# Stages of two attention heads, and transposes of four norm blocks, at one place between weight tiles

## The chip, the core and the metric

The kernel runs on one core of a Trainium2 chip. TensorE (PE in the profile, PEld its weight loads) multiplies, VectorE (DVE) and ScalarE (ACT) work on tiles, and SyncE (SP) issues the transfers; each engine takes its own instructions strictly in the order in which the program lists them. The metric is the device time of one execution in microseconds. Before the change it is 2163.51 us, the median of three runs (2163.22 to 2163.67).

## What is computed

Two layers of a decoder trunk, on 256 tokens of width 2048, in float32. Cut to what matters:

```python
for l in range(2):
    h = rms_norm(x, norm_mix[l])
    proj = h @ w_in[l]
    o_a = diff_attention(...)       # 4 heads: (softmax(q1 k1) - lam * softmax(q2 k2)) @ v, then an RMS norm over each head
    o_b = forgetting_attention(...) # 6 heads, logits += cumsum(log f)[t] - cumsum(log f)[s]
    o_c = latent_attention(...)     # 6 heads, q and kv from low-rank parts
    x = x + concat(o_a, o_b, o_c) @ w_out[l]
    h = rms_norm(x, norm_ffn[l])
    x = x + square(relu(h @ w_ff_up[l])) @ w_ff_down[l]
```

## The kernel before

Every weight matrix passes once through the chip in tiles of 128 rows and up to 1024 columns. `load_w` (L187) fetches a tile (`wraw`), rounds it on ACT to a high part (`whi`, L194) and leaves the rest on DVE as a low part (`wlo`, L195); there are three buffers for each part. A product of float32 quality is made of three passes on PE: high by high, high by the activations' low part, and low by high. For a tile of 1024 columns that is 12 matmuls of 512 columns, called `wo`, `dn` and so on after their accumulator; the products of one layer are, in order, the input projections (`mq`, `mkv`, `fv`, `fq`, `fk`, `dq`, `dk`, `dv`), the output projection (`wo`), and the two of the feed-forward part (`u`, `dn`).

All else is background work. A stage is a Python generator, cut by `yield` into portions. The class `Background` (L81) holds a queue of them. After each weight tile the program calls `bg.step()` (L100), which credits 1.25 units (never over 4 in hand) and runs one portion for each whole unit. So background work is written between weight tiles, and a scheduler below the program then places it on each engine, near where it was written. `bg.finish()` (L106) runs all that is left at once.

`side_by_side` (L111) joins several stages into one, two of them active: it takes a portion of the first, yields, takes one of the second, yields. It carries the heads: `latent_head` (L567) and `fox_head` (L652) have five portions each (scale; transposes of q and k, `qk`; scores `s` and their exponentials, `exps` L368; transposes of the probabilities, `pt`, from `transposed_p` L385; values `o`), `diff_maps` (L717) four (transposes `qk`; scores of the first map; scores of the second and their difference; `pt`). The last portion of a head ends the generator without a yield, so that it costs no unit.

The end of differential attention matters below. `diff_values` (L742) of a head makes its output `o` on PE; then, for each of the two row blocks, ACT squares it (L751) and DVE copies it to `osb` (L752). `diff_outputs` (L755) makes from the sums of squares of all four heads the norm's factors (`rsqrt_of` L212: eleven small DVE operations, `a_subln`, `y_subln`, `w_subln`), multiplies both `osb` (L760), transposes them on PE (`qk`), and splits the result to the last four heads' slots of `mix` (`split_to` L202). These slots are what the last four of the 16 weight tiles of the left half of `wo` multiply (`HEAD_ORDER` puts these heads last). The left half runs 12 tiles with `bg.step`, then `bg.finish()`, then the last four (L786 to L790):

```python
out_columns(left, w_left, 0, HALF, 0, N_EARLY, bg.step)
bg.finish()
out_columns(left, w_left, 0, HALF, N_EARLY, 16)
```

`Norm.columns` (L277) prepares the activations of the next product: squares on ACT for the norm, then for each pair of 128-column blocks four transposes into one bank (`xt`) and the split of both blocks, with a yield after each pair.

Of the kernel before, what the change touches and what calls it, by code (L numbers as in the profile page):

```python
# [19 lines left out]
P = 128  # L20
D_MODEL = 2048
SEQ = 256
# [5 lines left out]
NH_A, NH_B, NH_C = 4, 6, 6  # L28
# [52 lines left out]
class Background:  # L81

    def __init__(self):
        self.tasks = deque()
        self.rate = 1.25
        self.due = 0.0
# [11 lines left out]
    def step(self):  # L100
        self.due = min(self.due + self.rate, 4.0)
        while self.due >= 1.0:
            self.due -= 1.0
            self.one()

    def finish(self):  # L106
        while self.tasks:
# [2 lines left out]

def side_by_side(stages, width=2):  # L111

    rest, active = deque(stages), []
    while rest or active:
        while rest and len(active) < width:
            active.append(rest.popleft())
        for a in list(active):
            try:
                next(a)
                yield  # L120
            except StopIteration:
                active.remove(a)


@with_exitstack
def trunk_kernel(ctx: ExitStack, tc: tile.TileContext, ins: dict, out: bass.AP):
# [10 lines left out]
    def acc_tile(name):  # L137
        return ps_acc.tile([P, 512], F32, tag="acc", name=name)

    def t_tile(name):  # L140
        return ps_t.tile([P, 512], F32, tag="t", name=name)

    def mm(out, lhsT, rhs, start, stop):
        nc.tensor.matmul(out, lhsT, rhs, start=start, stop=stop)  # L144

    bg = Background()
# [23 lines left out]
    x = cp.tile([P, NT, D_MODEL], F32, name="x")  # L170
# [10 lines left out]
    for j in range(4):  # L181
        h = cp.tile([P, SEQ], F32, name=f"half{j}")
# [16 lines left out]
    def parts_tile(tag, name):  # L199
        return hp.tile([P, 2, 2, SEQ], F32R, tag=tag, name=name)  # L200

    def split_to(dst, src, gain):  # L202

        if gain is None:
            nc.scalar.activation(dst[:, 0, :], src, AF.Copy)
            nc.vector.tensor_tensor(dst[:, 1, :], src, dst[:, 0, :], ALU.subtract)
        else:
            nc.scalar.activation(dst[:, 0, :], src, AF.Copy, scale=gain)  # L208
            nc.vector.scalar_tensor_tensor(dst[:, 1, :], src, gain, dst[:, 0, :], ALU.mult, ALU.subtract)


    def rsqrt_of(ss, n, spans, name):  # L212
        a = sp.tile([P, 48], F32, tag="rs_a", name=f"a_{name}")
        y = sp.tile([P, 48], F32, tag="rs_y", name=f"y_{name}", bufs=3)
        w = sp.tile([P, 48], F32, tag="rs_w", name=f"w_{name}")
        for sl, d in spans:
            nc.vector.tensor_scalar(a[:, sl], ss[:, sl], 1.0 / d, EPS, ALU.mult, ALU.add)
        nc.vector.tensor_scalar(y[:, :n].bitcast(I32), a[:, :n].bitcast(I32), -0.5, RSQRT_SEED, ALU.mult, ALU.add)
        for _ in range(3):
            nc.vector.tensor_tensor(w[:, :n], y[:, :n], y[:, :n], ALU.mult)  # L220
            nc.vector.scalar_tensor_tensor(w[:, :n], w[:, :n], -0.5, a[:, :n], ALU.mult, ALU.mult)
            nc.vector.scalar_tensor_tensor(y[:, :n], w[:, :n], 1.5, y[:, :n], ALU.add, ALU.mult)
        return y
# [45 lines left out]
    class Norm:  # L269
# [7 lines left out]
        def columns(self, c0, n):  # L277
            for q in range(c0 // 512, (c0 + n) // 512):
                for t in range(NT):
                    junk = sp.tile([P, 512], F32, tag="junk", name="junk")  # L280
                    nc.scalar.activation(junk, x[:, t, q * 512:(q + 1) * 512], AF.Square, accum_out=self.sums[:, t, q:q + 1])
            for k in range(c0 // P, (c0 + n) // P, 2):
                b = acc_tile("xt")
                for i in range(2):
                    for t in range(NT):
                        transpose_block(b[:, i * SEQ + t * P:i * SEQ + (t + 1) * P], x[:, t, (k + i) * P:(k + i + 1) * P])
                h = parts_tile("ht", "ht")
                for i in range(2):
                    split_to(h[:, i], b[:, i * SEQ:(i + 1) * SEQ], self.gain[:, k + i:k + i + 1])
                self.h.append(h)  # L290
                yield

        def scale(self):

# [59 lines left out]
    def transpose_block(dst, src):  # L354
        nc.tensor.transpose(dst, src, ident)  # L355
# [45 lines left out]
    def heads_transposed(pairs):  # L401

        b = t_tile("qk")
        for i, blocks in enumerate(pairs):
            for t in range(NT):
                transpose_block(b[:, i * SEQ + t * P:i * SEQ + (t + 1) * P], blocks[t])
        return b
# [12 lines left out]
    h = norm.h  # L420

    for l in range(DEPTH):
# [18 lines left out]
        def mix_slot(i):  # L441

            return mix[i // 2][:, i % 2]
# [150 lines left out]

        mix_slots()
        bg.add(latent_rotation(), side_by_side([latent_head(i) for i in range(NH_C)]))


# [76 lines left out]
        def fox_half(s):  # L675
            qk = [ap.tile([P, 768], F32, tag="mid", name=f"fqk{s}{t}", bufs=4) for t in range(NT)]
            ss = sp.tile([P, 12], F32, tag="ss_f", name="ss_f")
            for a, g in enumerate(("fq", "fk")):
                if l == 0:
                    cols = slice((2 * s + a) * 512, (2 * s + a + 1) * 512)  # L680
                    nc.sync.dma_start(x[:, :, cols], ins["x"][:, :, cols])
                w_in_group(l, f"{g}{s}", h, scaled_copy(lambda t: qk[t][:, a * 384:(a + 1) * 384]))
                for t in range(NT):
                    head_sums(ss[:, t * 6 + 3 * a:t * 6 + 3 * a + 3], qk[t][:, a * 384:(a + 1) * 384], 3, P)
            rf = rsqrt_of(ss, 12, [(slice(0, 12), P)], f"fox{s}")
            bg.add(side_by_side([fox_head(i, qk, rf) for i in range(3 * s, 3 * s + 3)]))
# [30 lines left out]
        def diff_maps(i):  # L717
# [16 lines left out]
            dpT[i] = transposed_p(p1)  # L734

        bg.add(diff_rotation(), side_by_side([diff_maps(i) for i in range(NH_A)]))
        w_in_group(l, "dv", h, scaled_copy(lambda t: dv[t]))

# [3 lines left out]
        def diff_values(i):  # L742
            pT = dpT[i]
            o = t_tile("o")
            vi = slice(i * P, (i + 1) * P)
            mm(o[:, :P], pT[:, :P], dv[0][:, vi], True, True)
            mm(o[:, P:SEQ], pT[:, P:2 * P], dv[0][:, vi], True, False)
            mm(o[:, P:SEQ], pT[:, 2 * P:], dv[1][:, vi], False, True)
            for t in range(NT):
                junk = sp.tile([P, 512], F32, tag="junk", name="junk")  # L750
                nc.scalar.activation(junk[:, :P], o[:, t * P:(t + 1) * P], AF.Square, accum_out=ss_o[:, t * 4 + i:t * 4 + i + 1])  # L751
                nc.vector.tensor_copy(osb[t][:, vi], o[:, t * P:(t + 1) * P])  # L752
            yield

        def diff_outputs():  # L755
            ro = rsqrt_of(ss_o, 8, [(slice(0, 8), P)], "subln")
            yield
            for t in range(NT):
                o3 = osb[t].rearrange("p (n d) -> p n d", d=P)
                nc.vector.tensor_tensor(o3, o3, ro[:, t * 4:(t + 1) * 4].unsqueeze(2).broadcast_to([P, 4, P]), ALU.mult)  # L760
            yield
            for i in range(0, NH_A, 2):
                b = heads_transposed([[osb[t][:, (i + a) * P:(i + a + 1) * P] for t in range(NT)] for a in range(2)])
                for a in range(2):
                    split_to(mix_slot(12 + i + a), b[:, a * SEQ:(a + 1) * SEQ], g_o)
                yield

        bg.add(*(diff_values(i) for i in range(NH_A)), diff_outputs())


        if l + 1 < DEPTH:
# [2 lines left out]
        h = norm.h  # L774
# [3 lines left out]
        def out_columns(accs, w, c0, width, first, last, step=lambda: None):  # L778
            per = 1024 // width
            for i in range(first, last, per):  # L780
                hi, lo = load_w(w(i // per), 1024)
                for k in range(per):
                    product_x(accs, heads[i + k], hi, lo, k * width, i + k == 0, i + k == 15)
                step()
# [8 lines left out]
        for q in range(2):  # L793
            c0 = HALF + q * 512
# [96 lines left out]
        banks = [t_tile, acc_tile]  # L891
# [86 lines left out]
def build(shapes):  # L978
    import concourse.bacc as bacc

    nc = bacc.Bacc("TRN2", target_bir_lowering=False, num_devices=1, dynamic_dma_scratch_size=1024)
    ins = {k: nc.dram_tensor(f"in_{k}", s, F32, kind="ExternalInput").ap() for k, s in shapes.items()}
    out = nc.dram_tensor("out_0", (SEQ, D_MODEL), F32, kind="ExternalOutput").ap()
    with tile.TileContext(nc) as tc:
        trunk_kernel(tc, ins, out)
    return nc
# [9 lines left out]
```

## Time and profile before

| | before |
|---|---|
| median of three runs | 2163.51 us |
| the profiled execution's own time | 2162.75 us |
| its span, first to last instruction | 2161.0 us |
| PE busy | 2147.7 us, 99% of the span |
| PE weight loads busy | 1858.4 us, 86% |
| DVE busy | 1358.7 us, 63% |
| ACT busy | 1082.2 us, 50% |
| DMA, mean share of 16 engines | 57.4% (weights) |

The time of an execution and the span of its trace differ by 1.75 us that lie around the first and the last instruction. Busy time of PE counts a matmul from its start to a modelled end, and matmuls overlap in the pipeline, so the pace of PE is read from the starts of its rows, not from their lengths.

### The profile page before, as it was taken

The numbers are of one execution on the slowest core, as the hardware profiler recorded it, in microseconds if no ns is written. First come the engines' busy times: TensorE is split into PE (matmuls) and PEld (weight loads), VectorE is DVE, ScalarE is ACT, GpSimd is POOL, SyncE is SP. The second block draws the span as 40 slices with busy tenths as digits, with TensorE's granted clock in tenths as the row PEclk, the third lists the DMA queues.
The fourth block names the chain that finished last, engine by engine and source line by source line (L and its number), as shares of the span: only waits on it lengthen the run. The fifth ranks groups of instructions, "written<-read, shape, count | busy, mean of one in ns | idle before, by whom it ended". The sixth has DMA issues, their size and how long they took to land. (4 is left out here: it accounts for less than half of the span.)

```text
span 2161.0 us, 29221 instructions
## 1 busy us (share of the span) xinstructions
PE 2147.7 (99%) x11080; PEld 1858.4 (86%) x11080; DVE 1358.7 (63%) x2160; ACT 1082.2 (50%) x1603; POOL 13.5 (1%) x16
## 2 busy tenths in 40 slices
PE   9999999999999999999999999999999999999999
PEld 7999888888888888888899998888888888888887
DVE  7876676656565655555668667766555555655654
ACT  6655555544454444544566555555444444444442
POOL 2000000000000000000000000000000000000000
PEclk9999999999999999999999999999999999999999
DMA  8545545555566566655555455455565666655654
GB/s 277 173 140 179 163 150 181 186 193 189 193 189 193 185 196 193 189 192 190 184 161 171 137 182 172 146 184 185 186 195 185 195 193 189 193 189 191 193 190 153
DMA packets 115420, 395.68 MB, mean 183 GB/s; under 512 B 13008, under 2 KB 13136, under 8 KB 115280
## 3 DMA queue, kind: packets, MB, share of 16 engines
q1 hardware_dynamic: 115280, 393.83, 57.4%
q8 instruction: 86, 1.41, 0.3%
q14 instruction: 54, 0.44, 0.1%
HBM read 391.68 MB, written 2.10 MB: 182 GB/s over the span
## 5 line engine op out<-in xcount | busy, mean ns | idle before, releaser
L195 DVE TENSOR_TENSOR wlo<-wraw,whi 128x1024 fp32r<-128x1024 f32 (+3 forms) x773 | 909.0, 1178 | 707.5 <-ACT whi L194 694.8
L194 ACT ACTIVATE whi<-wraw 128x1024 fp32r<-128x1024 f32 (+3 forms) x773 | 788.5, 1021 | 954.7 <-PE dn L144 354.5
L144 PE MATMUL u<-ht,whi 128*128 128x512 f32 x2048 | 513.0, 392 | 0.0
L144 PE MATMUL dn<-whi,g 128*128 128x512 f32 x2048 | 510.5, 390 | 0.4 <-ACT whi L194 0.4
L144 PEld LDWEIGHTS dn<-whi,g 128*128 128x128 f32 x2048 | 383.1, 188 | 79.7 <-issue 1.2
L144 PEld LDWEIGHTS u<-ht,whi 128*128 128x128 f32 x2048 | 369.2, 189 | 66.7
L144 PEld LDWEIGHTS u<-ht,wlo 128*128 128x128 f32 x2048 | 279.4, 190 | 20.0
L144 PE MATMUL u<-ht,wlo 128*128 128x256 f32 x2048 | 285.5, 282 | 0.0
L144 PE MATMUL dn<-wlo,g 128*128 128x512 f32 x1024 | 277.3, 389 | 0.0
L144 PEld LDWEIGHTS dn<-wlo,g 128*128 128x128 f32 x1024 | 192.3, 188 | 40.0
L144 PE MATMUL wo<-whi,mix 128*128 128x512 f32 x512 | 138.1, 400 | 0.5 <-ACT mix L208 0.5
L144 PEld LDWEIGHTS wo<-whi,mix 128*128 128x128 f32 x512 | 94.3, 188 | 19.4 <-ACT mix L208 0.9
L323 DVE TENSOR_TENSOR x<-dn,x 128x512 f32<-128x512 f32 x128 | 79.7, 684 | 26.1 <-PE dn L144 26.1
L144 PE MATMUL wo<-wlo,mix 128*128 128x512 f32 x256 | 74.1, 390 | 0.0
L375 ACT ACTIVATE p<-p,nm 128x128 f32<-128x128 f32 x80 | 35.8, 448 | 44.6 <-DVE nm L374 44.6
L144 PEld LDWEIGHTS wo<-wlo,mix 128*128 128x128 f32 x256 | 48.0, 188 | 10.4
L144 PE MATMUL fq<-whi,ht 128*128 128x384 f32 x256 | 53.7, 349 | 0.0
L827 DVE TENSOR_TENSOR relu<-u,relu 128x256 f32<-128x256 f32 x128 | 53.4, 418 | 0.0
L144 PE MATMUL fk<-whi,ht 128*128 128x384 f32 x256 | 51.7, 343 | 0.0
L144 PE MATMUL fv<-whi,ht 128*128 128x384 f32 x256 | 51.1, 340 | 0.0
L826 ACT COPY relu<-u 128x256 f32<-128x256 f32 x128 | 45.9, 359 | 0.0
L828 DVE SCALAR_TENSOR_TENSOR relu<-relu,rsb 128x512 f32<-128x512 f32 x64 | 44.3, 692 | 2.3
(252 smaller groups left out, 1671.5 us busy)
## 6 DMA issues: line engine op xcount, KB each, us to landing
wraw<-in_w_up SPq DMA_DIRECT2D x256, 512.0 KB, 4.2
wraw<-in_w_down_a SPq DMA_DIRECT2D x128, 512.0 KB, 4.2
wraw<-in_w_down_b SPq DMA_DIRECT2D x112, 512.0 KB, 3.6
wraw<-in_w_out_a SPq DMA_DIRECT2D x32, 512.0 KB, 3.6
wraw<-in_w_out_b SPq DMA_DIRECT2D x32, 512.0 KB, 3.5
wraw<-in_w_fv SPq DMA_DIRECT2D x32, 384.0 KB, 3.1
wraw<-in_w_fq SPq DMA_DIRECT2D x32, 384.0 KB, 3.2
wraw<-in_w_fk SPq DMA_DIRECT2D x32, 384.0 KB, 3.1
```

Source lines behind the costliest of these rows:

```text
L144: nc.tensor.matmul(out, lhsT, rhs, start=start, stop=stop)
L194: nc.scalar.activation(hi[:, cols], raw[:, cols], AF.Copy)
L195: nc.vector.tensor_tensor(lo[:, cols], raw[:, cols], hi[:, cols], ALU.subtract)
L323: nc.vector.tensor_tensor(cols, acc, cols, ALU.add)
L375: nc.scalar.activation(p[:, cols], p[:, cols], AF.Exp, bias=nm[:, i:i + 1], scale=-1.0, accum_out=z[:, i:i + 1])
L826: nc.scalar.copy(r[:, cols], u[i][:, SEQ:])
L827: nc.vector.tensor_tensor(r[:, cols], u[i][:, :SEQ], r[:, cols], ALU.add)
L828: nc.vector.scalar_tensor_tensor(r, r, 0.0, rsb2, ALU.max, ALU.mult)
```

## The change

A background step now runs a round. `side_by_side` takes one portion of every active stage and then yields how many there were; `Background.step` takes what a step yields off the credit (1 for a stage that yields nothing), so that a round of two costs two units and the credit may fall below zero. A stage whose generator ends is found by the default that `next` returns, and the round in which it ends is paid like the others. The values of the four differential heads, which stood in the queue one by one, go through `side_by_side` too, and lose their yield. `Norm.columns` transposes four blocks into two banks in one step of two units and then splits all four. Nothing is added to or taken from the arithmetic.

```diff
     def step(self):
         self.due = min(self.due + self.rate, 4.0)
         while self.due >= 1.0:
-            self.due -= 1.0
-            self.one()
+            self.due -= self.one() or 1.0
...
 def side_by_side(stages, width=2):
     rest, active = deque(stages), []
     while rest or active:
         while rest and len(active) < width:
             active.append(rest.popleft())
-        for a in list(active):
-            try:
-                next(a)
-                yield
-            except StopIteration:
-                active.remove(a)
+        n = len(active)
+        active = [a for a in active if next(a, active) is not active]
+        yield n
...
-            for k in range(c0 // P, (c0 + n) // P, 2):
-                b = acc_tile("xt")
-                for i in range(2):
+            for k in range(c0 // P, (c0 + n) // P, 4):
+                banks = [acc_tile("xt") for _ in range(2)]
+                for i in range(4):
                     for t in range(NT):
-                        transpose_block(b[:, i * SEQ + t * P:i * SEQ + (t + 1) * P], x[:, t, (k + i) * P:(k + i + 1) * P])
-                h = parts_tile("ht", "ht")
-                for i in range(2):
-                    split_to(h[:, i], b[:, i * SEQ:(i + 1) * SEQ], self.gain[:, k + i:k + i + 1])
-                self.h.append(h)
-                yield
+                        transpose_block(banks[i // 2][:, i % 2 * SEQ + t * P:i % 2 * SEQ + (t + 1) * P],
+                                        x[:, t, (k + i) * P:(k + i + 1) * P])
+                for j, b in enumerate(banks):
+                    h = parts_tile("ht", "ht")
+                    for i in range(2):
+                        split_to(h[:, i], b[:, i * SEQ:(i + 1) * SEQ], self.gain[:, k + 2 * j + i:k + 2 * j + i + 1])
+                    self.h.append(h)
+                yield 2
...
                 nc.vector.tensor_copy(osb[t][:, vi], o[:, t * P:(t + 1) * P])
+            return
             yield
...
-        bg.add(*(diff_values(i) for i in range(NH_A)), diff_outputs())
+        bg.add(side_by_side([diff_values(i) for i in range(NH_A)]), diff_outputs())
```

What this does to the order of the instructions is shown at three places; numbers behind names are buffer numbers, and line numbers of the changed kernel are one or two off.

The first is PE in layer 1, at the end of differential attention, from the next to last stage of values on (`wo` are the weight tiles' matmuls, `o` a head's values, `qk` the transposes of the normed outputs `osb`). Before:

```order
L144 MATMUL wo<-whi,mix_4_10281 128x512 x8
L144 MATMUL wo<-wlo,mix_4_10281 128x512 x4
L144 MATMUL o<-dv_12152,pT 128x128 x2
L144 MATMUL o<-dv_12153,pT 128x128
L144 MATMUL wo<-whi,mix_5_10282 128x512 x8
L144 MATMUL wo<-wlo,mix_5_10282 128x512 x4
L144 MATMUL wo<-whi,mix_5_10282 128x512 x8
L144 MATMUL wo<-wlo,mix_5_10282 128x512 x4
L355 MATMUL qk<-cst,osb_12368 128x128 x2
L355 MATMUL qk<-cst,osb_12369 128x128
```

And with the change:

```order
L142 MATMUL o<-dv_12152,pT 128x128 x2
L142 MATMUL o<-dv_12153,pT 128x128
L142 MATMUL wo<-whi,mix_5_10282 128x512 x8
L142 MATMUL wo<-wlo,mix_5_10282 128x512 x4
L142 MATMUL o<-dv_12152,pT 128x128 x2
L142 MATMUL o<-dv_12153,pT 128x128
L142 MATMUL o<-dv_12152,pT 128x128 x2
L142 MATMUL o<-dv_12153,pT 128x128
L355 MATMUL qk<-cst,osb_12368 128x128 x2
L355 MATMUL qk<-cst,osb_12369 128x128
```

Before, two weight tiles (24 matmuls) stand between the last head's values and the transposes; now the values of the last two heads stand directly ahead of the transposes. In layer 0 the same two tiles have gone from between them.

The second is DVE at the same place in layer 1 (`osb` are the copies, `wlo` the low part of a weight tile, `subln` the small operations of the norm's factors). Before:

```order
L752 COPY osb_12368<-o 128x128
L752 COPY osb_12369<-o 128x128
L195 TENSOR_TENSOR wlo<-wraw,whi 128x1024
L752 COPY osb_12368<-o 128x128
L752 COPY osb_12369<-o 128x128
L217 TENSOR_SCALAR a_subln<-ss_o 128x8
L218 TENSOR_SCALAR y_subln<-a_subln 128x8
L220 TENSOR_TENSOR w_subln<-y_subln 128x8
L221 SCALAR_TENSOR_TENSOR w_subln<-w_subln,a_subln 128x8
L222 SCALAR_TENSOR_TENSOR y_subln<-w_subln,y_subln 128x8
```

And with the change:

```order
L193 TENSOR_TENSOR wlo<-wraw,whi 128x1024
L752 COPY osb_12368<-o 128x128
L752 COPY osb_12369<-o 128x128
L752 COPY osb_12368<-o 128x128
L752 COPY osb_12369<-o 128x128
L215 TENSOR_SCALAR a_subln<-ss_o 128x8
L216 TENSOR_SCALAR y_subln<-a_subln 128x8
L218 TENSOR_TENSOR w_subln<-y_subln 128x8
```

One `wlo` now stands ahead of four copies instead of two, and the norm's eleven small operations follow them; the second `wlo`, which stood among the eleven, has moved ahead.

The third is PE in layer 1 at the second pair of differential heads (`s` are the scores, `pt` the transposes of the probabilities). Before:

```order
L144 MATMUL s<-kT,half_102 128x128
L144 MATMUL s<-kT,half_102 128x256
L144 MATMUL wo<-whi,mix_3_10280 128x512 x8
L144 MATMUL wo<-wlo,mix_3_10280 128x512 x4
L144 MATMUL s<-kT,half_106 128x128
L144 MATMUL s<-kT,half_106 128x256
L144 MATMUL wo<-whi,mix_3_10280 128x512 x8
L144 MATMUL wo<-wlo,mix_3_10280 128x512 x4
L355 MATMUL pt<-cst,p 128x128 x3
L144 MATMUL wo<-whi,mix_4_10281 128x512 x3
L355 MATMUL pt<-cst,p 128x128
```

And with the change:

```order
L142 MATMUL s<-kT,half_102 128x128
L142 MATMUL s<-kT,half_102 128x256
L142 MATMUL s<-kT,half_106 128x128
L142 MATMUL s<-kT,half_106 128x256
L142 MATMUL wo<-whi,mix_4_10281 128x512 x8
L142 MATMUL wo<-wlo,mix_4_10281 128x512 x4
L355 MATMUL pt<-cst,p 128x128
L142 MATMUL wo<-whi,mix_4_10281 128x512
L355 MATMUL pt<-cst,p 128x128 x2
L142 MATMUL wo<-whi,mix_4_10281 128x512 x7
L142 MATMUL wo<-wlo,mix_4_10281 128x512 x2
L355 MATMUL pt<-cst,p 128x128
```

The scores of the two heads, which stood on either side of a weight tile, now stand together; one tile separates them from the transposes of the first head as it separated the second head's scores from the first head's transposes before, and the transposes of the second head come within that next tile.

## Rows read from the trace of the kernel before

**Rows 1.** The page: busy time by engine, clock granted in 40 slices.

```profile
PE 2147.7 (99%) x11080; PEld 1858.4 (86%) x11080; DVE 1358.7 (63%) x2160; ACT 1082.2 (50%) x1603; POOL 13.5 (1%) x16
...
PEclk9999999999999999999999999999999999999999
```

**Rows 2.** Waits of PE, whole span: total us, times, longest.

```profile
PE fv L144 <- DVE wlo L195: 0.8, 2, 0.4
...
PE pt L355 <- DVE p L731: 0.6, 3, 0.2
```

**Rows 3.** Timeline of PE, 136 to 148 us: start, length, what, count.

```profile
138.69 0.49 PE L355 MATMUL pt<-cst,p 128*128 128x128 f32 x3
...
141.11 1.47 PE L144 MATMUL o<-pT,mv 128*128 128x256 f32 x8
142.33 1.66 PE L144 MATMUL fv<-whi,ht 128*128 128x384 f32 x8
...
146.60 0.83 PE L144 MATMUL cum<-cst,lfx 128*128 128x128 f32 x6
```

**Rows 4.** Timeline of all engines, layer 1, end of differential attention.

```profile
1382.80 0.83 PE L144 MATMUL o<-dv,pT 128*128 128x128 f32 x6
1383.38 2.09 PE L144 MATMUL wo<-whi,mix 128*128 128x512 f32 x8
1383.72 0.28 ACT L751 ACTIVATE junk<-o 128x128 f32<-128x128 f32 x1 [0.58 <-PE o L144]
...
1384.31 0.28 DVE L752 COPY osb<-o 128x128 f32<-128x128 f32 x1
...
1385.03 0.29 DVE L752 COPY osb<-o 128x128 f32<-128x128 f32 x1 [0.43 <-ACT junk L751]
...
1385.24 0.16 DVE L217 TENSOR_SCALAR a_subln<-ss_o 128x8 f32<-128x8 f32 x1
...
1387.90 0.16 DVE L220 TENSOR_TENSOR w_subln<-y_subln 128x8 f32<-128x8 f32 x1
...
1388.49 1.29 DVE L760 TENSOR_TENSOR osb<-osb,y_subln 128x512 f32<-128x512 f32 x2
1389.24 0.44 PE L355 MATMUL qk<-cst,osb 128*128 128x128 f32 x2
...
1389.84 0.88 PE L355 MATMUL qk<-cst,osb 128*128 128x128 f32 x6 [0.17 <-DVE osb L760]
...
1390.95 2.14 PE L144 MATMUL wo<-whi,mix 128*128 128x512 f32 x8 [0.24 <-ACT mix L208]
```

**Rows 5.** Timeline of PE, layer 0, the same place.

```profile
314.77 1.07 PE L144 MATMUL wo<-wlo,mix 128*128 128x512 f32 x4
315.98 0.44 PE L355 MATMUL qk<-cst,osb 128*128 128x128 f32 x2
316.58 0.87 PE L355 MATMUL qk<-cst,osb 128*128 128x128 f32 x6 [0.16 <-DVE osb L760]
317.69 1.65 PE L144 MATMUL wo<-whi,mix 128*128 128x512 f32 x6 [0.24 <-ACT mix L208]
```

**Rows 6.** Timeline of all engines, 93 to 106 us: two latent heads.

```profile
97.62 0.49 PE L355 MATMUL pt<-cst,p 128*128 128x128 f32 x3
...
98.05 0.96 DVE L195 TENSOR_TENSOR wlo<-wraw,whi 128x768 fp32r<-128x768 f32 x1 [0.39 <-ACT whi L194]
...
99.32 0.35 DVE L382 TENSOR_SCALAR p<-p,r 128x256 f32<-128x256 f32 x1
```

**Rows 7.** Timeline of PE, layer 1: one differential head's probabilities are late.

```profile
1374.36 0.94 PE L144 MATMUL wo<-whi,mix 128*128 128x512 f32 x3
1375.50 0.33 PE L355 MATMUL pt<-cst,p 128*128 128x128 f32 x1 [0.20 <-DVE p L731]
```

**Rows 8.** PE by form: first matmuls, and a common form: busy us, mean ns.

```profile
L144 PE MATMUL dn<-whi,g 128*128 128x512 f32 x2048 | 510.5, 390 | 0.4 <-ACT whi L194 0.4
...
L144 PE MATMUL warm<-zeros 128*128 128x512 bf16 x12 | 4.1, 512 | 1.2 <-DVE zeros L162 1.2
```

## Prediction

> **What bounds the kernel now.** I read the page first: PE is busy for 99% of the span, with the granted clock full in all 40 slices [rows 1], so only what lets PE pause or work less can move the time. PE's own list of waits comes next: it is short, its largest entries for this change being 0.6 us for the transposes of probabilities and 0.8 us for a weight tile's low part [rows 2]. A pause is read more fully from starts in the timeline, since the modelled end of a matmul covers some 0.16 us of a pause. The pace for that: a matmul of 512 columns lasts 390 ns [rows 8], and four of them 1.07 us [rows 5], so they start (1.07 - 0.39) / 3 = 0.227 us apart; small ones start about 0.11 us apart.
>
> **What a place costs.** The change takes about 28 places away, 150 before and 122 after, counted over the whole order of PE. Three transposes and the 12 matmuls of a tile take 141.11 - 138.69 = 2.42 us, and 24 matmuls without a place in between 146.60 - 142.33 = 4.27 us, 2.135 for 12 [rows 3]. That leaves 0.285 us for three transposes, no more than their pace of 0.11. Going from a tile to background work and back costs PE nothing that can be seen; 28 places fewer I cost at 0. The bound, 0.05 us each, is 1.4 us of gain. What counts is how long PE then waits for DVE and ACT.
>
> **The tail of differential attention** is the main term. By the units of the program, a differential head took three before, as its last portion was free, and takes four now; four heads make 16 instead of 12. With six for the rotation, four for the values and four for the outputs the queue needs 30 units instead of 26, and eight tiles of `dv` and 12 of `wo` give 20 x 1.25 = 25. The order shows the effect in both layers: the two tiles between the last values and the transposes of the normed outputs are gone, and nothing on PE hides the norm.
>
> The chain is timed from layer 1 [rows 4]. The last head's values start at 1382.80 and take PE 0.58 (the next tile starts at 1383.38). ACT squares from 1383.72, DVE copies at 1384.31 and 1385.03, and the norm begins at 1385.24: 2.44 us after the values started, in which a square and a copy take turns every 0.72 us. With two heads there are two more turns, since both engines take their work in order: +1.44, so 3.88. The eleven small operations run at the pace of the last three, (1388.49 - 1387.90) / 3 = 0.197 us: 2.17. From the first of the two multiplications at 1388.49 the transposes start after 0.75, those that need the second after 1.35, and the next tile starts at 1390.95, 2.46 later. Sum: 3.88 + 2.17 + 2.46 = 8.51 us from the values to the next tile. PE's own work in it is 2 x 0.58 for the values and 8 x 0.11 for the transposes, 2.04 in all: it pauses for 6.47 us.
>
> Before, PE already paused there. In layer 0 four matmuls start at 314.77 and are due to end 0.91 later, at 315.68, but the transposes start at 315.98 (0.30); two of these last until 316.20, the next start at 316.58 (0.38); six until 317.24, the tile at 317.69 (0.45) [rows 5]. That is 1.13 us, and layer 1 restarts at the same distances (1389.24, 1389.84, 1390.95) [rows 4]. The change thus adds 6.47 - 1.13 = 5.34 us in each layer, **10.7 us** for two. Bounds: if the second head's squares and copies hide behind its own matmuls but for 0.58 us, 4.48 each, 9.0 in all; if the second head's 2.44 us stand wholly behind the first's, 6.34 each, 12.7. I take the turns, because the rows show that square and copy wait for each other.
>
> At this pause a rule speaks for more. The trace has no pause of PE of 5 us, and the granted clock never falls in it [rows 1]. The Trainium skill, page "TensorE: Matmul & The Clock Gate", section "HAM oscillation — how this bites in real kernels", says that a long enough wait between bursts of matmuls puts the clock back to half, and that the next burst starts at half speed; no run here shows it yet. By the rows alone the sum stays as it is; by the rule it is larger, and that is the first rival below.
>
> **Scores and probabilities.** In the order, six rounds (five in layer 0, one in layer 1) have both heads' scores, one weight tile, and then the transposes of both heads' probabilities within the next eight or so matmuls. Before, the second head had more time. In the pair of latent heads at 97 us the second head's probabilities are ready at 99.32 + 0.35 = 99.67, behind a low part of 0.96 us on DVE; the first head's transposes start at 97.62 [rows 6]. PE would now ask for the second's between 97.95 (directly behind) and 99.4 (eight matmuls of 0.178 later). It waits 0.3 us at the later place, and at the earlier one, where the order has no low part in the way, 99.67 - 0.96 - 97.95 = 0.76. I take 0.5, the middle: 6 x 0.5 = 3.0 us. Against that, four waits of the differential heads go, two in each layer: three matmuls from 1374.36 should end at 1375.04, the transpose starts at 1375.50, 0.46 us late [rows 7]; 4 x 0.46 = 1.8 us. Net **+1.2 us**, between -1.8 (they go, none comes) and +4.6 (six of 0.76, none goes).
>
> **The norm's transposes** I cost at nothing. They are in no entry of PE's waits, and in the changed order 12 or more matmuls, 2.7 us, stand between a round of them and the next. Their four splits reach DVE and ACT in one burst; if that cover failed, the wait would appear as one for a low part, of the 0.4 us in [rows 2]. The number of transfers and their order do not change; SP and POOL have nothing moved.
>
> **Sum.** 2162.75 (the profiled execution's own time) + 10.7 + 1.2 = 2174.65 us. The median of the three runs is 0.76 above that execution, so the forecast is **2175.4 us**.
>
> **Rivals.** *The clock falls in the pause.* Two pauses of about 5 us come where none was over some 1 us before. The first 12 matmuls of the kernel, after a still PE, last 512 ns against 390 for the same columns later [rows 8]: 12 x 0.122 = 1.5 us lost, and if the whole 4.1 us of that stretch ran at half speed, 2.05. Against it: the clock row shows no fall anywhere, the start included, so the loss there may have another cause. Twice 1.5 to 2.05 on top of the forecast gives 2178.4 to 2179.5. The rule of the Trainium skill cited above would have it so. Chance 0.22.
>
> *The low parts come late.* Two heads' exponentials, differences and scalings reach DVE at once, and the low part of a weight tile queues behind them; every matmul behind it on PE then waits. Such a wait lasts up to 0.4 us now [rows 2]. There are 18 rounds of paired scores in both layers; if every second one costs 0.4, that is 3.6 us: 2179.0. Against it: three buffers let DVE run two tiles ahead. Chance 0.12.
>
> *Faster.* Places are what costs: PE saves 28 x 0.05 = 1.4 us, the four late transposes (1.8) go and no new wait comes, and the tail is covered after all because ACT and DVE finish the first pair of heads early and the second pair overlaps PE's work. It decides at a tail that adds under 1.6 us per layer; with none added the time is 2160.3. Against it: the order has no tile left in the tail, and the small operations alone need 2.17 us. Chance 0.03.
>
> *The rounds do little.* If the order on the chip had other work of PE in the tail, or the norm's chain were half as long, the added pause would be 1 to 2 us per layer: about 2167. Chance 0.05.
>
> **The numbers.** Forecast 0.58, clock 0.22, late low parts 0.12, little 0.05, faster 0.03. A measurement of this kernel tells about 0.2%, 4.3 us, from no change. The first three cases are slower by more than that: 0.92; the fourth is the same: 0.05; faster 0.03. The range takes in the bounds: low, 2163.51 + 9.0 - 1.8 = 2170.7; high, 2163.51 + 12.7 + 4.6 = 2180.8, which also covers the rivals at 2179. The likeliest case alone reaches about as far, since its bounds set the range.
>
> **What would show it.** In the profile after: between the last values and the next `wo` tile of each layer, PE's starts stand 8.5 us apart with DVE's eleven small operations in the middle without a `wlo` among them; the granted clock there is 1.00 (forecast) or lower (first rival); PE's wait for `osb` heads its list of waits. Waits for the second head's probabilities appear at six places, of 0.3 to 0.8 us; waits for `wlo` stay at two or so. It would be wrong if the tail's two pauses differ from 5.3 us added, or if much time goes where no row of before shows a wait.

## The result and the profile after

The changed kernel takes 2175.76 us, the median of six runs (2174.42 to 2177.01), against 2163.69 us of the kernel before (2163.22 to 2164.53): 12.07 us more, a ratio of 1.0055 with a 95% interval of 1.0044 to 1.0066. The forecast was 2175.4 us. As the section on the reasons shows, the number is nearer than its parts were.

The page of the profile after, in the line that answers to [rows 1] (its own time is 2174.42 us, the fastest of the six, and its span 2172.6 us):

```profile
PE 2150.6 (99%) x11080; PEld 1861.4 (86%) x11080; DVE 1355.9 (62%) x2160; ACT 1081.2 (50%) x1603; POOL 12.0 (1%) x16
```

PE stays at 99%, and its busy time has grown by 2.9 us although it executes the same 11080 matmuls: some of them took longer. The clock row reads as in [rows 1], full tenths everywhere, because a slice is 54 us long; a fall of some microseconds can't be seen in it, and the mean clock of the run, 0.997, is the first hint.

PE's wait for `osb`, the normed outputs, before, the columns as in [rows 2]:

```profile
PE qk L355 <- DVE osb L760: 0.3, 2, 0.2
```

And its waits after:

```profile
PE qk L355 <- DVE osb L761: 9.8, 2, 4.9
...
PE fv L142 <- DVE wlo L193: 0.8, 2, 0.4
...
PE pt L355 <- DVE p L381: 0.2, 1, 0.2
```

The wait for `osb`, 0.3 us before, is now 9.8 us in two times, and stands at the head. The wait of `fv` for the low part is unchanged. The three waits for the probabilities of the differential heads, 0.6 us in all [rows 2], are gone, and one of 0.2 us for those of another head (L381) has come.

Where the time went is read from two landmarks in each layer: the first matmul of `wo` and the first of `u`. Timeline of PE before (start, length, what):

```profile
272.67 1.04 PE L144 MATMUL wo<-whi,mix 128*128 128x512 f32 x3
...
375.05 0.84 PE L144 MATMUL u<-ht,whi 128*128 128x512 f32 x3
...
1346.08 1.05 PE L144 MATMUL wo<-whi,mix 128*128 128x512 f32 x3
...
1448.41 0.84 PE L144 MATMUL u<-ht,whi 128*128 128x512 f32 x3
```

And after:

```profile
273.38 0.84 PE L142 MATMUL wo<-whi,mix 128*128 128x512 f32 x3
...
381.37 0.84 PE L142 MATMUL u<-ht,whi 128*128 128x512 f32 x3
...
1352.43 0.81 PE L142 MATMUL wo<-whi,mix 128*128 128x512 f32 x2
...
1460.15 0.62 PE L142 MATMUL u<-ht,whi 128*128 128x512 f32 x2
```

The output projection took 102.38 and 102.33 us and takes 107.99 and 107.72: 5.61 and 5.39 more, 11.0 of the 11.6 us by which the span grew. The tail of differential attention lies in these stretches; all other attention, the norms and the feed-forward part share the remaining 0.6 us.

The tail itself, in layer 0, all engines; it answers to [rows 4, 5]:

```profile
314.76 1.50 PE L142 MATMUL o<-dv,pT 128*128 128x128 f32 x12
...
315.69 0.28 ACT L751 ACTIVATE junk<-o 128x128 f32<-128x128 f32 x1 [0.57 <-PE o L142]
...
316.29 0.28 DVE L752 COPY osb<-o 128x128 f32<-128x128 f32 x1
...
316.60 0.28 ACT L751 ACTIVATE junk<-o 128x128 f32<-128x128 f32 x1 [0.55 <-DVE osb L752]
...
316.87 0.27 ACT L751 ACTIVATE junk<-o 128x128 f32<-128x128 f32 x1
317.00 0.55 DVE L752 COPY osb<-o 128x128 f32<-128x128 f32 x2 [0.43 <-ACT junk L751]
...
318.20 0.16 DVE L215 TENSOR_SCALAR a_subln<-ss_o 128x8 f32<-128x8 f32 x1
...
320.40 1.29 DVE L761 TENSOR_TENSOR osb<-osb,y_subln 128x512 f32<-128x512 f32 x2
...
321.15 2.14 PE L355 MATMUL qk<-cst,osb 128*128 128x128 f32 x8 [4.89 <-DVE osb L761]
...
323.21 2.99 PE L142 MATMUL wo<-whi,mix 128*128 128x512 f32 x8
...
326.04 1.07 PE L142 MATMUL wo<-wlo,mix 128*128 128x512 f32 x4
```

Both heads' values start at 314.76, the norm at 318.20 (3.44 us; the forecast had 3.88), its eleven small operations stand together until 320.40 (2.20; forecast 2.17), the transposes start at 321.15, and the next tile at 323.21. From values to tile it is 8.45 us, and 8.51 were forecast. But the last two steps differ from before: from the first transpose to the tile 2.06 us against 1.71, and eight matmuls of the tile take 326.04 - 323.21 = 2.83 us where eight at 0.227 are 1.82.

The same stretch by windows of the timeline (us, then busy us and instructions of PE, PEld, DVE, ACT, POOL, then the granted clock, DMA share and GB/s):

```profile
318.00:320.00 2.00, 0.00 (x0) 0.00 (x0) 1.69 (x11) 0.00 (x0) 0.00 (x0) 0.58 0.53 209
320.00:322.00 2.00, 0.85 (x3) 0.55 (x4) 1.62 (x4) 0.00 (x0) 0.00 (x0) 0.50 0.00 0
...
324.00:326.00 2.00, 2.00 (x8) 1.59 (x7) 1.19 (x3) 0.66 (x2) 0.00 (x0) 0.71 0.00 0
```

PE has no instruction at all from 318 to 320, and there the granted clock falls to its lower level, 0.50 of full, 1.2 instead of 2.4 GHz. It is still low while the transposes and the first five matmuls of the tile run; the mean of 0.71 in the last window puts its rise at about 325.2.

Layer 1, where PE pauses as long, is a little different (PE's rows, then windows with the columns as above):

```profile
1393.76 1.50 PE L142 MATMUL o<-dv,pT 128*128 128x128 f32 x12
...
1402.21 2.83 PE L142 MATMUL wo<-whi,mix 128*128 128x512 f32 x8
1404.88 1.07 PE L142 MATMUL wo<-wlo,mix 128*128 128x512 f32 x4
```

```profile
1398.00:1400.00 2.00, 0.00 (x0) 0.00 (x0) 1.76 (x8) 0.00 (x0) 0.00 (x0) 1.00 0.05 21
1400.00:1402.00 2.00, 1.79 (x8) 1.34 (x8) 0.69 (x2) 0.32 (x1) 0.00 (x0) 0.59 0.00 0
1402.00:1404.00 2.00, 2.00 (x7) 1.45 (x6) 1.50 (x4) 1.50 (x4) 0.00 (x0) 0.56 0.00 0
```

From values to tile it is 8.45 us again. Here the clock is full to the end of the pause and falls only at about 1400.4, when the transposes have begun; it rises at about 1403.8, and the tile's first eight matmuls take 2.67 us. By these windows the clock was low for some 6.8 us in layer 0 and 3.4 us in layer 1. So the first rival came true on top of the forecast.

### The profile page after: what moved, and what is told of

It reads as the page before. It is cut to its first block, busy times and chain, and to the rows that moved or that the text cites. A ratio compares the mean times of both kernels' runs of the same rounds, so it can differ in the third digit from the quotient of the medians.

```text
span 2172.6 us, 29222 instructions
## 1 busy us (share of the span) xinstructions
PE 2150.6 (99%) x11080; PEld 1861.4 (86%) x11080; DVE 1355.9 (62%) x2160; ACT 1081.2 (50%) x1603; POOL 12.0 (1%) x16
## 4 chain that ended last, share of the span: by engine, by line
PE 88%; DVE 3%; ACT 1%; issue 1%; DVEq 0%; ACTq 0%
PE u L142 33%; PE dn L142 32%; PE wo L142 7%; PE fq L142 2%; PE fk L142 2%; PE dk L142 2%; PE dq L142 2%; PE fv L142 2%; PE s L142 1%; PE mq L142 1%; DVE wlo L193 1%; PE o L142 1%; PE qk L355 1%; PE mkv L142 1%; PE qup L142 1%
```

## The experiments

Nine kernels were run after the result. The theory was that the whole loss lies in the uncovered norm and in the clock that falls in its pause; the main rival, that rounds of two heads cost by bursts on DVE and ACT all over attention.

**The last portion free again.** The changed kernel, but a round in which both heads end yields nothing, so that a differential head needs three units again. The values, whose one round is also their last, then cost no unit at all: the queue needs 22 units, less than the 26 of the kernel before, and 25 are credited:

```diff
         n = len(active)
         active = [a for a in active if next(a, active) is not active]
-        yield n
+        if active:
+            yield n
```

> The changed kernel, but a round in which both heads end costs nothing again, as a head's last portion did before the change: the differential heads need 12 units, not 16. In the order three weight tiles stand again between the values and the transposes of the normed outputs. Theory (the uncovered norm at the end of differential attention and the clock that falls in its pause make the loss): PE's pause there is under 1.5 us, the granted clock is 1.00 throughout, and the time is 2163 to 2165.5 us. Rival (the rounds themselves cost, by bursts on DVE and ACT all over attention): it stays above 2170 us.

It takes 2160.36 us (2159.86 to 2160.83, 11 runs), a ratio to the kernel before of 0.9985 (0.9976 to 0.9993): the loss is gone, and it is 3.3 us faster than the kernel before. Its last tile and transposes in layer 1, on PE:

```profile
1384.40 1.07 PE L143 MATMUL wo<-wlo,mix 128*128 128x512 f32 x4
1385.59 0.44 PE L356 MATMUL qk<-cst,osb 128*128 128x128 f32 x2
1385.78 0.71 PE L143 MATMUL wo<-whi,mix 128*128 128x512 f32 x2
1386.33 0.82 PE L356 MATMUL qk<-cst,osb 128*128 128x128 f32 x6
1386.91 1.64 PE L143 MATMUL wo<-whi,mix 128*128 128x512 f32 x6
```

The four matmuls from 1384.40 are due to end at 1385.31; the transposes start 0.28 us later, two matmuls fill the wait for the second `osb`, and early tiles' matmuls follow the last transposes, so that no wait for `mix` is left, where the kernel before paused 0.3, 0.38 and 0.45 us [rows 5]. All stages still run in rounds, only the price of the last one differs, so rounds as such are not what costs. The time came out below the expected 2163 to 2165.5 us, in part because the pauses that the kernel before had in its own tail go too. One part of the expectation failed: the clock is not 1.00 throughout. At the kernel's start, where PE waits 1.69 us for a high part, it falls, and its mean is 0.57 from 8 to 12 us, where the trace of the kernel before has 1.00. This has no part in the tail.

**The kernel before, made to pay.** No rounds, but one unit more for each differential head:

```diff
             dpT[i] = transposed_p(p1)
+            yield
```

> The kernel before, with heads taken by turns, and one yield more at the end of each differential head, so that its last portion costs a unit. No rounds at all. Theory: the values of two heads stand directly ahead of the transposes in both layers, PE pauses some 5 us in each, the clock falls, and the time is 2174 to 2177.5 us, 5.2 of pause and 1.2 of clock for each layer. Rival (rounds cost): 2163.5 to 2165 us.

It takes 2175.26 us (2174.89 to 2176.42), ratio 1.0054 (1.0042 to 1.0067), the same as the whole change, within the expected range. PE in layer 0:

```profile
314.35 1.50 PE L144 MATMUL o<-dv,pT 128*128 128x128 f32 x12
320.73 2.14 PE L355 MATMUL qk<-cst,osb 128*128 128x128 f32 x8 [4.88 <-DVE osb L761]
322.80 3.78 PE L144 MATMUL wo<-whi,mix 128*128 128x512 f32 x8
326.38 1.15 PE L144 MATMUL wo<-wlo,mix 128*128 128x512 f32 x4
```

The two heads' values, 6.38 us to the transposes, and a tile whose first eight matmuls take 3.58 us, with a granted clock of 0.50 from 320 to 326 us. Four units more in the queue, one for each head, make the whole loss without any round; this is the run that decides between the theory and its rival.

**Rounds everywhere but there.** The changed kernel with differential attention as before: heads by turns, values one by one.

```diff
-        bg.add(diff_rotation(), side_by_side([diff_maps(i) for i in range(NH_A)]))
+        bg.add(diff_rotation(), by_turns([diff_maps(i) for i in range(NH_A)]))
...
-        bg.add(side_by_side([diff_values(i) for i in range(NH_A)]), diff_outputs())
+        bg.add(*(diff_values(i) for i in range(NH_A)), diff_outputs())
```

(`by_turns` is the old `side_by_side`, and `diff_values` has its yield again.)

> The changed kernel, with differential attention alone as before: its heads by turns, its values one by one; rounds in the latent and the forgetting heads and four norm blocks at once stay. Theory: the tail has its two covering tiles again, and the rest of the change costs about 1 us: 2164 to 2165.5 us. Rival (bursts of two heads cost over all of attention, at least half of the loss): 2168 us or more.

It takes 2163.88 us (2162.68 to 2164.15), ratio 1.0000 (0.9991 to 1.0008). PE at the tail of layer 1 is the one of before:

```profile
1389.48 1.07 PE L155 MATMUL wo<-wlo,mix 128*128 128x512 f32 x4
1390.69 0.44 PE L368 MATMUL qk<-cst,osb 128*128 128x128 f32 x2
1391.29 0.88 PE L368 MATMUL qk<-cst,osb 128*128 128x128 f32 x6 [0.16 <-DVE osb L773]
1392.40 2.14 PE L155 MATMUL wo<-whi,mix 128*128 128x512 f32 x8 [0.24 <-ACT mix L219]
```

The pauses of 0.3, 0.38 and 0.45 us are back and nothing else: rounds in the twelve other heads of each layer and in the norms cost nothing that can be measured, a little less than the expected 1 us.

**The norm's blocks alone.** The kernel before with `Norm.columns` of the change, and with the line in `Background.step` that takes its two units off the credit:

```diff
-            self.due -= 1.0
-            self.one()
+            self.due -= self.one() or 1.0
...
-            for k in range(c0 // P, (c0 + n) // P, 2):
+            for k in range(c0 // P, (c0 + n) // P, 4):
...
-                yield
+                yield 2
```

> The kernel before, with the transposes of four norm blocks at one place and nothing else of the change. Theory (a place costs PE nothing, and the norm's stages are covered by weight tiles): no change, 2163.0 to 2164.2 us. Rival (merging places gains): 1 us or more faster.

It takes 2163.01 us (2162.43 to 2163.71) against 2163.76, ratio 0.9997 (0.9988 to 1.0005): no change that the interval can tell. The medians differ by 0.75 us, with ten places fewer in its order; a gain of up to 2.6 us lies within the interval.

**Matmuls in the pause.** Two kernels fill the changed kernel's pause with matmuls whose result nobody reads, to hold the clock. First 18 matmuls of 512 columns on zeros:

```diff
+            fill = t_tile("fill")
+            for _ in range(18):
+                mm(fill, zeros[:, :P], zeros, True, True)
             ro = rsqrt_of(ss_o, 8, [(slice(0, 8), P)], "subln")
```

> The changed kernel with 18 matmuls of 512 columns of zeros on PE, 3.9 us of work, between the last values and the transposes, where PE pauses 5.05 us. Theory (the pause is a wait for DVE, and 1.2 us of each layer's loss is the clock that falls in it): the clock stays at 1.00, the distance from the values to the next tile falls from 8.45 to about 8.1 us, the tile after it takes 2.0 us again and not 2.83 for its first eight matmuls; time 2173 to 2174 us, 2.4 us less than the changed kernel. Rival (a fallen clock costs nothing, as PE waits for DVE anyway): 2175.8 us, with the same distance.

It takes 2174.22 us (2172.35 to 2174.92), 1.5 us less than the changed kernel instead of 2.4. In the profile the clock holds in layer 0 but falls in layer 1, after the filler (PE's row of the next tile, then windows, columns as above):

```profile
1401.44 3.46 PE L142 MATMUL wo<-whi,mix 128*128 128x512 f32 x8 [0.24 <-ACT mix L206]
```

```profile
1400.00:1402.00 2.00, 1.59 (x10) 1.16 (x9) 0.85 (x3) 0.90 (x3) 0.00 (x0) 0.96 0.00 0
1402.00:1404.00 2.00, 2.00 (x6) 1.52 (x6) 1.18 (x3) 0.81 (x2) 0.00 (x0) 0.50 0.00 0
```

The mean of 0.96 puts the fall at the end of the first window, at about 1401.8, when the transposes are done and the tile has begun. The five executions fall into two groups, which the median hides: 2172.35 and 2172.96 us, with a mean clock of 1.000, and 2174.22, 2174.61 and 2174.92 us, with 0.999; the profiled one is of the second. So the filler of zeros seems to have held the clock in both layers in two of five; no trace of such an execution was kept.

Then 40 matmuls of 256 columns on real data, half a microsecond longer in all:

```diff
+            for _ in range(40):
+                mm(fill[:, :SEQ], c_q[:, :P], c_q, True, True)
```

> The changed kernel with 40 matmuls of 256 columns on real data, some 4.4 us, in the tail's pause, instead of the 18 of zeros (with these the clock held in layer 0 and fell in layer 1, for 2174.2 us). Theory (the fallen clock costs 1.2 us in each layer, and matmuls in the pause hold it): the clock is full in both layers, the distance from the values to the next tile stays 8.1 us, 2172.8 to 2173.8 us. Rival (the clock has no part in the loss): 2175 to 2176 us.

It takes 2172.63 us (2172.40 to 2172.75), a little less than expected, and its clock is 1.000. PE in layer 0:

```profile
315.29 1.50 PE L142 MATMUL o<-dv,pT 128*128 128x128 f32 x12
316.62 4.53 PE L142 MATMUL fill<-c_q 128*128 128x256 bf16 x40
321.68 0.44 PE L355 MATMUL qk<-cst,osb 128*128 128x128 f32 x2 [0.53 <-DVE osb L764]
322.28 0.87 PE L355 MATMUL qk<-cst,osb 128*128 128x128 f32 x6 [0.17 <-DVE osb L764]
323.39 2.14 PE L142 MATMUL wo<-whi,mix 128*128 128x512 f32 x8 [0.24 <-ACT mix L206]
325.37 1.08 PE L142 MATMUL wo<-wlo,mix 128*128 128x512 f32 x4
```

From the values at 315.29 to the tile at 323.39 it is 8.10 us now, and the tile's eight matmuls take 1.98 us. The pause remains, filled with work for nobody, and the median is 3.13 us below that of the changed kernel, 1.6 us for each fall. The two traces show 2.3 us of it: the output projections last 106.79 and 106.65 us here, against 107.99 and 107.72, so that the falls cost 1.20 and 1.07 us. In layer 0 this is 0.35 us from values to tile and 0.85 in the tile. A fall can cost more: the kernel before, made to pay, needs 3.58 us for the eight matmuls that take 2.83 in the changed kernel. As the profiled execution of the changed kernel is its fastest, the rest of the 3.13 us may be longer falls in the others; that was not shown. The two fillers differ in their data, in the number and width of their matmuls and in the pause that they leave (1.0 and 0.5 us before the transposes); which of these held the clock every time was not told apart.

**More units.** The changed kernel with 1.75 units for a tile from `dv` to the end of the covering tiles, 35 for the 30 needed:

```diff
+        bg.rate = 1.75
         w_in_group(l, "dv", h, scaled_copy(lambda t: dv[t]))
...
         bg.finish()
+        bg.rate = 1.25
```

> The changed kernel, with 1.75 units for a weight tile instead of 1.25 from the dv product to the end of the twelve covering tiles: 35 units for the 30 that the differential stages cost. In the order two to three tiles stand between the last values and the transposes again. Theory (what the rounds did was to run out of units): the pause at the tail is under 1 us, the clock is full, 2161 to 2164.5 us. Rival (the rounds of two heads are what loses): above 2170 us.

It takes 2161.51 us (2160.95 to 2161.96), ratio 0.9989 (0.9980 to 0.9998). All of the change's rounds, priced as in the change, are in it; only the budget differs. The same edit with 1.5 units, in the kernel before:

> The kernel before, with 1.5 units for a tile from the dv product to the end of the twelve covering tiles; no rounds. Theory (what made the changed kernel with a free last portion faster than the one before, 2160.4 against 2163.7 us, is the third covering tile in the tail, which takes away the pauses of 1.1 us in each layer, and the earlier probabilities): 2161 to 2162 us. Rival (that gain is of the rounds): 2163.5 us.

It takes 2161.49 us (2160.82 to 2161.86), ratio 0.9989 (0.9980 to 0.9998), with no round at all: 30 units are credited here for the 26 needed. So 2.3 of the 3.3 us that the free last portion gains over the kernel before are to be had from a larger budget alone; what part of this is the covered tail and what part the earlier probabilities was not told apart. The other 1.1 us, which the two intervals leave open, were not traced.

**Both remedies.** Free last portions and 1.5 units:

> Both remedies: rounds whose last portion is free, and 1.5 units for a tile from the dv product to the end of the covering tiles. The free portion alone gave 2160.4 us, with a pause of 0.3 us left at each tail. Theory (only pauses of PE can still be gained): 2159.5 to 2160.6 us, no more than 0.8 us below the free portion alone. Rival (earlier stages bring DVE's bursts against the weight tiles' low parts): 2161 us or more.

It takes 2161.09 us (2160.26 to 2161.84), ratio 0.9988 (0.9979 to 0.9997), not faster than the free portion alone: each output projection is shorter by 1.84 and 0.75 us, but its start comes later, by 1.18 us in layer 0 and by 1.57 us in layer 1 (there counted from the first `u` of layer 0). The rival was right here by its number; that DVE's bursts are the reason was not shown. The fastest of all these kernels is the changed one with the last portion free.

## Why the prediction came out right, and which of its steps did not

**The place costs nothing**: right as far as can be measured. The norm's blocks alone, with ten places fewer, and the rounds outside differential attention change nothing beyond their intervals, which reach 1.1 to 2.6 us to either side.

**The tail**: right in its place, its cause and nearly its size. The budget of units explains it, as the kernel before with one unit more for each head shows. Without the fall of the clock the distance from values to tile is 8.10 us in the run with data in the pause; less 2.04 of PE's own work and the 1.13 of before, 4.93 us were added in each layer, 9.9 in all, where 10.7 were forecast. The term that was too large is the second head's turn: +1.44 us were taken for two more turns of square and copy, and 3.44 - 2.44 = 1.00 was measured, since ACT squares the second head's first block while DVE still copies the first head's second. The turns themselves come of both engines reading one bank: the Trainium skill, page "PSUM — Partial Sum Buffer", section "Terms", says that two engines on the same bank at once are an error, reads included, so the program keeps them apart. The trace agrees: the first copy starts at 316.29, after the first square from 315.69 is over, and the second square at 316.60, after that copy; while the second head's first square at 316.87 runs beside the copies from 317.00, the first of which is the first head's. No run here has both read it at once.

**The clock**: the forecast, which held that it stays, was wrong, and the rival that it falls, given 0.22, was right in both layers. The page "TensorE: Matmul & The Clock Gate" of the Trainium skill, cited there, had it so; the trace now agrees for layer 0, with 0.50 granted in the pause and on into the next tile, while in layer 1 the burst began at full clock and the fall came some 0.2 us later. Its price was put at 1.5 to 2.05 us for each fall; by the medians it is 3.13 us for two, 1.57 each, and by the two traces 1.20 and 1.07. What spoke against this rival, that the clock row shows no fall at the start either, was weak: read matmul by matmul, the trace of the kernel before has its first seven starts 0.40 to 0.43 us apart and the last 0.22, while the row says full. The tile's starts during the fall in layer 0 are 0.43 us apart too. So that trace already held the lower pace.

**Scores and probabilities**: wrong in size. Six waits of 0.5 us less four of 0.46 were to add 1.2 us. The 0.46 was read at one place and taken for four: PE's list has three such waits, 0.6 us in all beyond the modelled ends [rows 2]. Timeline of PE after, at three of the late transposes:

```profile
145.03 0.30 PE L355 MATMUL pt<-cst,p 128*128 128x128 f32 x1 [0.16 <-DVE p L381]
...
304.18 1.18 PE L355 MATMUL pt<-cst,p 128*128 128x128 f32 x6
305.11 1.17 PE L142 MATMUL wo<-whi,mix 128*128 128x512 f32 x4
...
1382.25 1.08 PE L142 MATMUL wo<-wlo,mix 128*128 128x512 f32 x4
1383.34 0.33 PE L355 MATMUL pt<-cst,p 128*128 128x128 f32 x1
```

At 145.03 the trace gives 0.16 us of wait beyond the modelled end; the six transposes from 304.18 last 0.93 us instead of 0.66, 0.27 late; four matmuls from 1382.25 should end at 1383.16, and the transpose starts at 1383.34, 0.18 late; the last two are of differential heads. The waits are of 0.2 to 0.3 us and not of 0.5, while the waits for the differential heads (L731) are gone from PE's list. With the tail at 9.9 and the clock at 3.1 by the medians, all that is left of 12.1 us is 12.1 - 9.9 - 3.1 = -0.9 us: this term and every other one together, where +1.2 was forecast. What the term came to by itself was not separated, so not even its sign is known. The traces alone agree for the output projections: of the 11.0 us by which they grew, 9.9 and 2.3 leave -1.1.

So three errors, -0.8 in the tail, +3.1 in the clock and -2.1 in the rest, sum up to 0.2; another 0.2 is the median of the kernel before, 2163.69 us in six runs where the forecast stood on 2163.51. That the median lies 0.4 us from the forecast is partly luck: the forecast case, a pause at full clock, did not happen, and the loss by the clock hid what the other terms had too much. What was no luck is that the loss is a pause of PE at one place in each layer, read off the order and a chain of rows.

**The rivals that fell**: low parts did not come late (0.8 us of waits before and after). Fewer places brought no gain that could be measured. That the rounds do little is true only outside differential attention.

## What to carry to other kernels

Where background work is paced by a budget, count the units of the whole queue against the credit of the stretch that must hide it: here four units more put an eleven-operation chain behind PE's last covering work, and the engine that bounds the kernel paid for it. Look first at what stands between the last producer and its consumer in the order. A change of prices in such a pacer needs its rate set anew; with the rate or the price mended, the same rounds were faster than the kernel before, though a higher rate without rounds gained as much (2161.49 against 2161.51 us).

## What was not expected of the hardware

A pause of 5 us cost PE not only itself: the clock fell from 2.4 to 1.2 GHz, in layer 0 within the pause and in layer 1 just behind it, and was low for 3.4 to 6.8 us, while matmuls had come back: 1.57 us lost each time by the medians, 1.20 and 1.07 in the traces. It need not be 5 us: in the kernel with the free last portion the clock fell at the start, in a wait of 1.69 us that one of 0.28 us had preceded. The falls also differ between the layers of one run: with the filler of zeros one layer kept its clock and the other did not. The time was uneven: six runs of the changed kernel spread over 2.6 us, the five with data in the pause over 0.35 us. That this comes of the clock was not shown, as 27 runs of the kernel before spread over 2.3 us.
